# Streaming the projection matmuls from the last column to the first

## The chip, the core and the metric

One core of one Trainium2 chip runs the whole program in one launch. The metric is the device time of one execution in microseconds (us); lower is better. The kernel before was timed three times: 940.13, 941.47 and 944.43 us, median 941.47 us.

## The reference, cut to what matters

Two layers of a decoder trunk work on x, 256 tokens of 1024 features in float32. A layer is one wide projection of the normalised x, three token mixers, a gated merge, an output projection and a SwiGLU block:

```python
xn = rms(x, norm_mix_g)
z = xn @ w_in                                  # 1024 -> all heads and three gates
y_a, y_b, y_c = mlstm(z), sparse_attention(z), differential_attention(z)
merged = sum(sigmoid(gate_b) * (y_b @ w_branch[b]) for b in range(3))   # 512 -> 1024 each
x = x + merged @ w_out                         # 1024 -> 1024
g, u = split(rms(x, norm_ffn_g) @ w_gate_up)   # 1024 -> 2 x 2816
x = x + (silu(g) * u) @ w_down                 # 2816 -> 1024
```

Nearly all of the arithmetic is in the products with w_in, w_kv_up, w_branch, w_out, w_gate_up and w_down. They are called projections here.

## The kernel before

**Projections.** A float32 product is made of three passes of a faster matmul type (fp32r). Each operand is split into a high part (the fp32r copy) and a low part (the rest), and the passes are high by high, high by low and low by high, all summed in one PSUM tile. Two helpers issue these passes. `feat` (line 490) gives an output with features on partitions: the weight block of 128 columns is the stationary operand, and the 256 tokens of the activation's high or low part are streamed. `tok` (line 497) gives an output with tokens on partitions: 128 tokens of the activation are stationary, and 256, 332 or 512 weight columns are streamed. Every call writes the columns of a PSUM tile in the same order in which it streams them.

```python
490  def feat(ps, w, c0, a, first, last):
493      PE.matmul(ps, hi[:, c0:c0 + 128], a[:, 0, :], start=first, stop=False)
...
497  def tok(ps, w, c0, n, a, t, first, last):
501      PE.matmul(ps, a[:, 0, s], hi[:, c0:c0 + n], start=first, stop=False)
```

In the profile these are the matmuls `mm<-...`: `xg` and `fx` are the normalised inputs of a layer's two halves, `y` the mixers' outputs, `mg` the merged gates, `h` the SwiGLU activations and `ckv` the latent; `whi` and `wlo` are the two parts of a weight chunk. Matmuls named `at<-...` are the mixers' own (logits, transposes, values) and call neither helper.

**Weights.** `chunk` (line 472) loads up to 1024 columns of weights by one DMA on SyncE's queue into `raw`, makes `whi` on ScalarE and `wlo` on VectorE. Three buffers of each are in turn.

**Order of the work.** The kernel text only records operations. `Order.record` (line 149) notes for each which parts of which tiles it reads and writes, `Order.schedule` (line 177) lists them with a cost per instruction (`cost`, line 319) and a priority, and `Order.issue` (line 281) hands them to the engines in the order found. Line 288 issues every instruction, so every row of the profile has that line. A tile, or a part of one, is a `View` (line 20): a list of steps (index, rearrange, bitcast, broadcast) that `View.real` (line 94) applies to the real tile when the instruction is issued. `_next` (line 26) adds a step and passes on the shape and the range of columns.

**Readers of the PSUM tiles.** ScalarE or VectorE reads each finished `mm` tile as it always stands there, first column first; there are four such tiles in turn.

**Tiles of the second half.** In `norm` (line 509) the inputs of SwiGLU, `fx`, are written four feature blocks to one tile, each block as a high and a low part, so one tile has eight writers.

Of the kernel before, what the change touches and what calls it, by code (L numbers as in the profile page):

```python
# [19 lines left out]
class View:  # L20
    """A tile that is allocated when its first instruction is issued, or a part of it."""

# [65 lines left out]
    def bitcast(self, dtype):  # L88
        return self._next(("bitcast", dtype), self.shape, dtype)

    def to_broadcast(self, shape):
        return self._next(("bcast", shape), list(shape))

    def real(self, order):
        ap = order.tile_of(self.base)
        for s in self.steps:
            if s[0] == "get":
                ap = ap[s[1]]
            elif s[0] == "rearrange":
                ap = ap.rearrange(s[1], **s[2])  # L100
            elif s[0] == "bitcast":
                ap = ap.bitcast(s[1])
            else:
                ap = ap.to_broadcast(s[1])
        return ap
# [12 lines left out]
class Order:  # L118
    """Records instructions, puts them in an order by a list schedule, and issues them in it."""

# [186 lines left out]
def lat(a, b):  # L307
    """From the end of an instruction on engine a to the start of one on b that reads it, in us."""
    if a == b:
        return {"tensor": 0.0, "vector": 0.127, "scalar": 0.15, "gpsimd": 0.13, "sync": 0.0}[a]  # L310
    if b == "tensor":
        return 0.25
    return 0.2 if a == "tensor" or "gpsimd" in (a, b) else 0.14
# [5 lines left out]
def cost(op, views):  # L319
    """The time of an instruction in us."""  # L320
    n = max(math.prod(v.shape[1:]) for v in views)
    psum = any(v.base.psum for v in views)
    if op.eng == "tensor":
        n = math.prod(views[0].shape[1:])
        if op.fn == "transpose":
            return 0.109
        if views[1].dtype == BF16:
            return n / 1200
        if views[1].dtype == F32R:
            return max(n, 256) / 2400 + 0.0024  # L330
        return 0.216 if n <= 128 else 4 * n / 2400 + 0.0048
    if op.eng == "scalar":
        t = (0.05 if psum else 0.092) + n * 0.00084
        extra = [op.kw.get("scale"), op.kw.get("bias"), op.kw.get("accum_out")]
        return t + 0.093 * sum(isinstance(v, View) for v in extra)
    if op.eng == "vector":
        if op.fn == "reciprocal":
            return 0.05 + n * 0.0063
        t = 0.065 + n * (0.00052 if op.fn in ("tensor_copy", "tensor_scalar") and not psum else 0.00104)
        if op.fn == "scalar_tensor_tensor":  # L340
            t += 0.061 * isinstance(op.args[2], View)
        if op.fn == "tensor_tensor_reduce":
            t += 0.061 * isinstance(op.args[3], View)
        if op.fn == "tensor_scalar":
            t += 0.061 * sum(isinstance(v, View) for v in op.args[2:4])
        return t
    if op.eng == "gpsimd":
        if op.kw.get("op") == OP.pow:
            return 0.3 + n * 0.165
        if op.fn == "memset":  # L350
            return 0.04 + n * 0.0005
        if op.fn in ("tensor_scalar", "tensor_copy"):
            return 0.16 + n * (0.0037 if any(isinstance(v, View) for v in op.args[2:4]) else 0.00083)
        return 0.15 + n * 0.0021
    return 0.02 + 128 * n * 4 / 365e3
# [26 lines left out]
def plan():  # L382
    """The order in which a layer's weights are read: (array, row blocks, col blocks)."""
    seq = []
# [35 lines left out]
def kernel(ctx: ExitStack, tc: tile.TileContext, xT: bass.AP, wts: bass.AP, cst: bass.AP,  # L420
# [32 lines left out]

    # keeps TensorE's clock up until the first operands are there
    warm = S.tile([128, 256], BF16, name="warm")
# [34 lines left out]
    def feat(ps, w, c0, a, first, last):  # L490
        """ps [128 out, T] += w[:, c0:c0+128]^T a, three passes."""
        hi, lo = w
        PE.matmul(ps, hi[:, c0:c0 + 128], a[:, 0, :], start=first, stop=False)
        PE.matmul(ps, hi[:, c0:c0 + 128], a[:, 1, :], start=False, stop=False)
        PE.matmul(ps, lo[:, c0:c0 + 128], a[:, 0, :], start=False, stop=last)

    def tok(ps, w, c0, n, a, t, first, last):
        """ps [128 tok, n] += a[:, :, tile t]^T w[:, c0:c0+n], three passes."""
        hi, lo = w
        s = slice(t * 128, (t + 1) * 128)  # L500
        PE.matmul(ps, a[:, 0, s], hi[:, c0:c0 + n], start=first, stop=False)
        PE.matmul(ps, a[:, 0, s], lo[:, c0:c0 + n], start=False, stop=False)
        PE.matmul(ps, a[:, 1, s], hi[:, c0:c0 + n], start=False, stop=last)

    def rsqrt_cols(t, n):
        """t <- t ** -0.5 on GpSimd (t [128, n])."""
        G.tensor_tensor(t, t, mhalf[:, :n], op=OP.pow)

    def norm(gcol, wide, first=False):
        """x*g as hi/lo parts, 1/rms as token columns [128, 2] and as rows [128, T]."""  # L510
        xg = []
# [62 lines left out]
    def swap_halves(ap):  # L574
        """[128, h, 64] seen with the halves of the last axis exchanged, as two views."""
        return ap[:, :, 32:64], ap[:, :, 0:32]

    def rot(dst, z, nh, a, b):
        """dst = z * a + swap(z) * b over nh heads; a, b [128, 64]."""
        t2 = tmp([128, nh, 64], "rot")  # L580
        zh, zl = swap_halves(z)
        V.tensor_mul(t2[:, :, 0:32], zh, b[:, None, 0:32].to_broadcast([128, nh, 32]))
        V.tensor_mul(t2[:, :, 32:64], zl, b[:, None, 32:64].to_broadcast([128, nh, 32]))
        V.tensor_mul(dst, z, a[:, None, :].to_broadcast([128, nh, 64]))
        V.tensor_add(dst, dst, t2)
# [10 lines left out]
    def qk_heads(z, t, ab, dstT, query):  # L596
        """z [128 tok, 512] -> per-head RMS, RoPE, transposed into dstT[:, :, tile t]. Of a query
        the 1/rms is returned instead, as columns scaled by -1/sqrt(64), for softmax."""
        sq = tmp([128, 8, 64], "sq")
# [19 lines left out]
    def softmax(t, heads, qT, kT, bias, scale):  # L619
        """exp(logits - max) of the heads, [128 q, len(heads), nk], and its row sums."""  # L620
        n, nk = len(heads), 128 * (t + 1)
# [15 lines left out]
    def keyT(p, n, t):  # L637
        """p [128 q, n, nk] -> [128 keys, n, key tile, 128 q]."""
        ps = atps([128, n, t + 1, 128])
        for i in range(n):  # L640
            for kt in range(t + 1):
                PE.transpose(ps[:, i, kt, :], p[:, i, kt * 128:(kt + 1) * 128], ident)
        r = tmp([128, n, t + 1, 128], "pT")
        A.activation(r, ps, AF.Copy)
        return r

    def parts(dst, ps, t, g=None):
        """hi/lo of ps [128, 4, 128] (scaled by g[:, k]) into dst[:, k, :, tile t]."""
        s = slice(t * 128, (t + 1) * 128)
# [10 lines left out]
    for li in range(L):  # L660
# [12 lines left out]
        S.margin = True  # L673
        # mLSTM q and k: projection, causal convolution, silu
        mqk = []
# [19 lines left out]

        # DSA latent
        ps = [mmps([128, 256]) for _ in range(2)]
# [28 lines left out]

        # indexer projections and mLSTM gates
        ps2 = [mmps([128, 332]) for _ in range(2)]
# [26 lines left out]

        # index scores and the top-k mask
        bias = []
# [23 lines left out]

        # DSA queries
        def proj512():
# [13 lines left out]

        # DSA keys and values
        skT = S.tile([128, 4, T], F32, tag="qT", name="skT", bufs=4)
# [13 lines left out]

        # DSA attention
        y = [S.tile([128, 4, 2, T], F32R, tag="y", name=f"y{b}", bufs=3) for b in range(3)]
# [17 lines left out]

        # differential attention
        p = tmp([128, 2, 64], "lamp")
# [60 lines left out]

        # mLSTM gates
        mf = mif[:, :, 4:8]
# [33 lines left out]
        for t in range(2):  # L932
# [8 lines left out]
            if t == 1:  # L941
# [3 lines left out]
                ET.append(u)  # L945
        # (s tile, t tile) blocks: (0, 0), (1, 1), (0, 1)
        for b, (si, ti) in enumerate(((0, 0), (1, 1), (0, 1))):
# [5 lines left out]

        # mLSTM values and output gate
        p = proj512()
# [42 lines left out]

        # branch gates
        gt = []  # L1000
# [14 lines left out]
        S.margin = False  # L1015
        # branch projections, gated and merged
        mg = []
# [22 lines left out]

        # output projection
        for e in range(8):
# [5 lines left out]

        # SwiGLU
        xg, rcol, rB = norm(c[:, C_NF:C_NF + 8], True)  # L1050
# [50 lines left out]
def _layout(inp):  # L1101
    """The inputs in the kernel's layouts (moves only)."""
    src = {"in": inp["w_in"], "kv": inp["dsa_w_kv_up"], "out": inp["w_out"], "gu": inp["w_gate_up"],
# [42 lines left out]
```

## Time and profile before

| what | value |
|---|---|
| three runs | 940.13, 941.47, 944.43 us; median 941.47 us |
| the profiled execution's own time: span from first to last instruction (what lies around the span was not listed) | 942.7 us |
| TensorE matmul busy; weight loads busy | 933.5 us (99%); 888.6 us (94%) |
| VectorE, ScalarE, GpSimd busy | 678.6 us (72%), 534.0 us (57%), 103.3 us (11%) |
| matmul instructions, weight loads | 7154, 7154 |
| read from HBM, rate over the span | 158.27 MB, 169 GB/s |
| granted TensorE clock, mean | 1.000 |

The profile's busy time of an engine is the union of its instructions' times. Matmuls overlap each other, since a row's duration runs from the first column entering to the last one landing, so the pace of matmuls is read from the distance between their starts and not from their mean duration. The chain of waits is the path followed back from the last instruction; what stands in it sets the end.

### The profile page before, as it was taken

How to read it: one execution, taken by the hardware profiler on the slowest of the kernel's cores; microseconds unless marked ns; L12 is line 12 of the kernel's file. 1: busy time of each engine (PE TensorE's matmuls, PEld its weight loads, DVE VectorE, ACT ScalarE, POOL GpSimd, SP SyncE). 2: the span in 40 equal slices, each digit the busy share in tenths (PEclk: the TensorE clock that was granted, in tenths of full speed). 3: DMA queues.
4: the chain of work that ended last, by engine and by line, in shares of the span. 5: the costliest groups of instructions: out<-in, count | busy, mean ns of one | idle time of the engine just before them, and what ended most of it. 6: DMA issues, size and time to landing. Idle time of an engine off the chain costs nothing.

```text
span 942.7 us, 18057 instructions
## 1 busy us (share of the span) xinstructions
PE 933.5 (99%) x7154; PEld 888.6 (94%) x7154; DVE 678.6 (72%) x1268; ACT 534.0 (57%) x927; POOL 103.3 (11%) x149
## 2 busy tenths in 40 slices
PE   8999999999999999999999999999999999999998
PEld 7988779999999999999999787899999999999998
DVE  6889988765886666665578898796669866666553
ACT  5686667774365444444457767577644655445432
POOL 5002431110011000001110121213000300000000
PEclk9999999999999999999999999999999999999999
DMA  6655433445555555555555453333555555555663
GB/s 222 203 188 179 154 100 106 131 163 187 186 179 181 189 191 181 188 181 186 186 184 184 157 193 121 112 113 118 176 187 192 178 180 185 194 181 186 193 198 96
DMA packets 46821, 160.49 MB, mean 170 GB/s; under 512 B 5392, under 2 KB 7568, under 8 KB 46736
## 3 DMA queue, kind: packets, MB, share of 16 engines
q1 hardware_dynamic: 46736, 159.34, 52.0%
q8 instruction: 56, 0.92, 0.4%
q14 instruction: 29, 0.24, 0.1%
HBM read 158.27 MB, written 1.05 MB: 169 GB/s over the span
## 4 chain that ended last, share of the span: by engine, by line
PE 98%; DVE 1%; DMA 0%; issue 0%; SPq 0%; ACT 0%
PE mm L288 89%; PE at L288 8%; DVE e L288 0%; DMA x<-in_xT_dram 0%; DVE xg L288 0%; SPq L288 0%; DVE zr L288 0%; ACT xg L288 0%; DVE dn L288 0%; DVE x L288 0%; DVE rot L288 0%; ACT nsq L288 0%; DVE wlo L288 0%; DVE mn L288 0%; DVE cf L288 0%
## 5 line engine op out<-in xcount | busy, mean ns | idle before, releaser
L288 ACT ACTIVATE whi<-raw 128x1024 fp32r<-128x1024 f32 (+2 forms) x303 | 315.9, 1043 | 332.9 <-PE mm L288 212.0
L288 DVE TENSOR_TENSOR wlo<-raw,whi 128x1024 fp32r<-128x1024 f32 (+2 forms) x303 | 365.4, 1207 | 184.0 <-ACT whi L288 182.2
L288 PE MATMUL mm<-fx,whi 128*128 128x256 f32 x1408 | 249.6, 279 | 0.0
L288 PEld LDWEIGHTS mm<-fx,whi 128*128 128x128 f32 x1408 | 215.2, 188 | 0.0
L288 PE MATMUL mm<-xg,whi 128*128 128x256 f32 x1024 | 195.2, 289 | 1.8 <-DVE xg L288 1.8
L288 PE MATMUL mm<-fx,wlo 128*128 128x256 f32 x704 | 196.8, 280 | 0.0
L288 PEld LDWEIGHTS mm<-xg,whi 128*128 128x128 f32 x1024 | 163.7, 195 | 3.3 <-DVE xg L288 2.6
L288 PE MATMUL mm<-whi,xg 128*128 128x512 f32 (+2 forms) x512 | 150.3, 373 | 0.0
L288 PE MATMUL mm<-xg,wlo 128*128 128x256 f32 x512 | 148.0, 289 | 0.6 <-DVE wlo L288 0.6
L288 PEld LDWEIGHTS mm<-fx,wlo 128*128 128x128 f32 x704 | 132.0, 188 | 0.0
L288 PE MATMUL mm<-h,whi 128*128 128x256 f32 x704 | 124.5, 280 | 0.0
L288 PEld LDWEIGHTS mm<-h,whi 128*128 128x128 f32 x704 | 107.7, 188 | 0.0
L288 PEld LDWEIGHTS mm<-whi,xg 128*128 128x128 f32 x512 | 92.1, 188 | 14.7 <-issue 1.0
L288 PEld LDWEIGHTS mm<-xg,wlo 128*128 128x128 f32 x512 | 99.7, 195 | 1.2 <-DVE wlo L288 0.9
L288 PE MATMUL mm<-h,wlo 128*128 128x256 f32 x352 | 98.6, 280 | 0.0
L288 PE MATMUL mm<-wlo,xg 128*128 128x512 f32 (+2 forms) x256 | 95.6, 374 | 0.0
L288 PE MATMUL mm<-y,whi 128*128 128x256 f32 x384 | 67.9, 280 | 0.0
L288 PEld LDWEIGHTS mm<-h,wlo 128*128 128x128 f32 x352 | 66.4, 189 | 0.0
L288 POOL TENSOR_TENSOR nacc<-nacc,nsq 128x256 f32<-128x256 f32 x28 | 26.3, 939 | 361.1 <-ACT nsq L288 222.5
L288 PEld LDWEIGHTS mm<-y,whi 128*128 128x128 f32 x384 | 58.6, 187 | 0.0
L288 PEld LDWEIGHTS mm<-wlo,xg 128*128 128x128 f32 x256 | 48.3, 189 | 7.7 <-issue 0.7
L288 PE MATMUL mm<-y,wlo 128*128 128x256 f32 x192 | 53.6, 279 | 0.0
(193 smaller groups left out, 1095.4 us busy)
## 6 DMA issues: line engine op xcount, KB each, us to landing
raw<-in_wts_dram SPq DMA_DIRECT2D x279, 512.0 KB, 3.7
raw<-in_wts_dram SPq DMA_DIRECT2D x16, 384.0 KB, 3.9
raw<-in_wts_dram SPq DMA_DIRECT2D x4, 498.0 KB, 3.6
x<-in_xT_dram SPq DMA_DIRECT2D x4, 256.0 KB, 4.4
out_dram<-x SPq DMA_DIRECT2D x8, 128.0 KB, 3.4
row<-in_rows_dram SPq DMA_DIRECT2D x2, 388.0 KB, 5.7
raw<-in_wts_dram SPq DMA_DIRECT2D x2, 332.0 KB, 2.9
raw<-in_wts_dram SPq DMA_DIRECT2D x2, 256.0 KB, 3.8
```

Source lines behind the costliest of these rows:

```text
L288: getattr(getattr(nc, o.eng), o.fn)(*args, **kw)
```

## The change

`View` gets a method that turns the order of the columns round, and both helpers apply it to the streamed operand and to the PSUM output of all three passes. The stationary operands stay as they are. Streamed column j still lands in output column j; only the order in time goes from the last column to the first. Docstrings and comments are dropped as well, and no instruction is added or removed.

```diff
@@ class View
+    def back(self):
+
+        return self._next(("back",), self.shape)
@@ View.real
+            elif s[0] == "back":
+                ap = ap[:, ::-1]
@@ feat
         hi, lo = w
-        PE.matmul(ps, hi[:, c0:c0 + 128], a[:, 0, :], start=first, stop=False)
-        PE.matmul(ps, hi[:, c0:c0 + 128], a[:, 1, :], start=False, stop=False)
-        PE.matmul(ps, lo[:, c0:c0 + 128], a[:, 0, :], start=False, stop=last)
+        ps, a0, a1 = ps.back(), a[:, 0, :].back(), a[:, 1, :].back()
+        PE.matmul(ps, hi[:, c0:c0 + 128], a0, start=first, stop=False)
+        PE.matmul(ps, hi[:, c0:c0 + 128], a1, start=False, stop=False)
+        PE.matmul(ps, lo[:, c0:c0 + 128], a0, start=False, stop=last)
@@ tok
         hi, lo = w
         s = slice(t * 128, (t + 1) * 128)
-        PE.matmul(ps, a[:, 0, s], hi[:, c0:c0 + n], start=first, stop=False)
-        PE.matmul(ps, a[:, 0, s], lo[:, c0:c0 + n], start=False, stop=False)
-        PE.matmul(ps, a[:, 1, s], hi[:, c0:c0 + n], start=False, stop=last)
+        ps, h, l = ps.back(), hi[:, c0:c0 + n].back(), lo[:, c0:c0 + n].back()
+        PE.matmul(ps, a[:, 0, s], h, start=first, stop=False)
+        PE.matmul(ps, a[:, 0, s], l, start=False, stop=False)
+        PE.matmul(ps, a[:, 1, s], h, start=False, stop=last)
```

## Rows read from the trace of the kernel before

**Rows 1.** The page's first two parts: busy time of TensorE's matmuls and weight loads and of the other engines, with instructions; then the clock granted to TensorE in 40 equal slices of the span, in tenths (9 is 90% or more).

```profile
PE 933.5 (99%) x7154; PEld 888.6 (94%) x7154; DVE 678.6 (72%) x1268; ACT 534.0 (57%) x927; POOL 103.3 (11%) x149
...
PEclk9999999999999999999999999999999999999999
```

**Rows 2.** The page's chain that ended last, as shares of the span: by engine, and its first lines by line and tile.

```profile
PE 98%; DVE 1%; DMA 0%; issue 0%; SPq 0%; ACT 0%
PE mm L288 89%; PE at L288 8%; DVE e L288 0%; DMA x<-in_xT_dram 0%; DVE xg L288 0%; SPq L288 0%; DVE zr L288 0%; ACT xg L288 0%; DVE dn L288 0%; DVE x L288 0%; DVE rot L288 0%; ACT nsq L288 0%; DVE wlo L288 0%; DVE mn L288 0%; DVE cf L288 0%
```

**Rows 3.** All that TensorE waited for in the span: who, total us, times, longest us.

```profile
PE at L288 <- ACT warm L288: 2.3, 1, 2.3
PE mm L288 <- DVE xg L288: 1.8, 2, 1.2
PE mm L288 <- DVE wlo L288: 0.6, 1, 0.6
PE at L288 <- DVE mn L288: 0.3, 1, 0.3
```

**Rows 4.** The groups of projection matmuls over the span, each shape apart: stationary columns, streamed columns, count, then busy us and mean ns of one, then idle time before.

```profile
L288 PE MATMUL mm<-fx,whi 128*128 128x256 f32 x1408 | 249.6, 279 | 0.0
L288 PE MATMUL mm<-fx,wlo 128*128 128x256 f32 x704 | 196.8, 280 | 0.0
L288 PE MATMUL mm<-xg,whi 128*128 128x256 f32 x1024 | 195.2, 289 | 1.8 <-DVE xg L288 1.8
L288 PE MATMUL mm<-xg,wlo 128*128 128x256 f32 x512 | 148.0, 289 | 0.6 <-DVE wlo L288 0.6
L288 PE MATMUL mm<-h,whi 128*128 128x256 f32 x704 | 124.5, 280 | 0.0
L288 PE MATMUL mm<-whi,xg 128*128 128x512 f32 x384 | 124.0, 397 | 0.0
L288 PE MATMUL mm<-h,wlo 128*128 128x256 f32 x352 | 98.6, 280 | 0.0
L288 PE MATMUL mm<-wlo,xg 128*128 128x512 f32 x192 | 76.6, 399 | 0.0
L288 PE MATMUL mm<-y,whi 128*128 128x256 f32 x384 | 67.9, 280 | 0.0
L288 PE MATMUL mm<-y,wlo 128*128 128x256 f32 x192 | 53.6, 279 | 0.0
L288 PE MATMUL mm<-mg,whi 128*128 128x256 f32 x256 | 46.0, 283 | 0.0
L288 PE MATMUL mm<-mg,wlo 128*128 128x256 f32 x128 | 35.6, 283 | 0.0
L288 PE MATMUL mm<-whi,xg 128*128 128x332 f32 x64 | 15.1, 317 | 0.0
...
L288 PE MATMUL mm<-whi,xg 128*128 128x256 f32 x64 | 11.8, 283 | 0.0
L288 PE MATMUL mm<-whi,ckv 128*128 128x512 f32 x32 | 11.0, 404 | 0.0
...
L288 PE MATMUL mm<-wlo,xg 128*128 128x332 f32 x32 | 10.0, 313 | 0.0
L288 PE MATMUL mm<-wlo,xg 128*128 128x256 f32 x32 | 9.1, 283 | 0.0
...
L288 PE MATMUL mm<-wlo,ckv 128*128 128x512 f32 x16 | 6.4, 401 | 0.0
```

**Rows 5.** The chain of waits in order of time: start us, length us, what, how many matmuls. The first stretch has matmuls of 512 streamed columns, the other two (SwiGLU of layer 0 and of layer 1) of 256.

```profile
68.48 28.88 PE mm L288 x127
...
293.44 185.66 PE mm L288 x1574
...
756.74 181.89 PE mm L288 x1545
```

**Rows 6.** TensorE in order of time, the first of three matmuls of 332 columns, and then the first of the next three: start us, length us, instruction, count.

```profile
49.71 0.31 PE L288 MATMUL mm<-wlo,xg 128*128 128x332 f32 x1
...
50.16 0.31 PE L288 MATMUL mm<-wlo,xg 128*128 128x332 f32 x1
```

**Rows 7.** TensorE in order of time near the start, matmuls of 256 columns: the first row's two and one left out, the next row's two and one left out, and the one after them.

```profile
8.37 0.63 PE L288 MATMUL mm<-xg,whi 128*128 128x256 f32 x2
...
9.01 0.63 PE L288 MATMUL mm<-xg,whi 128*128 128x256 f32 x2
...
9.65 0.41 PE L288 MATMUL mm<-xg,whi 128*128 128x256 f32 x1
```

**Rows 8.** TensorE in order of time: four transposes of 128 columns, first those of `mM`, where the operand is one column repeated 128 times, then those of `yn`, where it is 128 different columns.

```profile
173.33 0.60 PE L288 MATMUL at<-K,mM 128*128 128x128 f32 x4
...
193.69 0.60 PE L288 MATMUL at<-K,yn 128*128 128x128 f32 x4
```

**Rows 9.** All engines in order of time at the start of layer 0's SwiGLU: the first matmuls that read `fx`, and VectorE's last write of a part of `fx`.

```profile
287.88 0.40 PE L288 MATMUL mm<-fx,whi 128*128 128x256 f32 x2
...
290.24 0.96 DVE L288 SCALAR_TENSOR_TENSOR fx<-x,col,fx 128x256 fp32r<-128x256 f32 x1
```

**Rows 10.** The costliest group of the page: ScalarE's making of `whi`, busy us and mean ns, then its idle time before and who ended most of it.

```profile
L288 ACT ACTIVATE whi<-raw 128x1024 fp32r<-128x1024 f32 (+2 forms) x303 | 315.9, 1043 | 332.9 <-PE mm L288 212.0
```

## The prediction

> **What bounds the kernel now.** I read the page's busy line first. TensorE's matmuls fill 99% of the span, its weight loads 94%, VectorE 72%, ScalarE 57% [rows 1]. A busy share alone proves little, since matmul rows overlap, so I went on to the chain that ended last: 98% of it is TensorE, 89% in the projection matmuls `mm` and 8% in the mixers' `at` [rows 2]. Then the waits: in the whole span TensorE waits 2.3 + 1.8 + 0.6 + 0.3 = 5.0 us for anyone [rows 3]. So the end is set by how fast TensorE gets through its stream, and nothing covers a change of pace there: a nanosecond more per projection matmul is a nanosecond more of the end, times their number.
>
> That number comes from the view that groups instructions by shape [rows 4]. Of 256 streamed columns there are 1408 + 704 + 1024 + 512 + 704 + 352 + 384 + 192 + 256 + 128 + 64 + 32 = 5760 matmuls, of 512 columns 384 + 192 + 32 + 16 = 624, and of 332 columns 64 + 32 = 96: 6480 in all. All of them come from the two helpers, so the change touches every one.
>
> The pace is read from the long unbroken stretches of the chain. 256 columns: 185.66 / 1574 = 118.0 ns and 181.89 / 1545 = 117.7 ns; I take 118.0. 512 columns: 28.88 / 127 = 227.4 ns [rows 5]. 332 columns: three from 49.71 to 50.16 us, 150 ns each [rows 6]. A straight line through the first and the last has (227.4 - 118.0) / 256 = 0.427 ns per column and 118.0 - 256 x 0.427 = 8.7 ns that come once per matmul; for 332 columns it gives 8.7 + 141.8 = 150.5 ns, which fits. So it is the number of streamed columns that sets the pace, with a small fixed part. The projections take 5760 x 118.0 + 624 x 227.4 + 96 x 150 ns = 679.7 + 141.9 + 14.4 = 836 us, near the chain's 89% of 942.7 us (839 us). [...]
>
> **The change part by part.** *Instructions, order and edits of text.* The docstrings and comments issue nothing. `back` adds a step to a view and passes on its shape and range of columns; the planner's cost is worked out from shapes, its dependences from ranges. So the order, the queues, the DMAs and the counts stay: 0 us, and no cover is needed, because nothing is added.
>
> *The arithmetic.* Streamed and output columns are turned round together, so each sum lands where it did, and the readers of PSUM start, as before, when the last pass ends. A reader that starts at column 0 doesn't start earlier because that column is written last. 0 us.
>
> *Waits.* Should a turned view be taken for more of its tile than it covers, a matmul would wait for all writers of that tile. For most operands that is so already, or all parts are long written. The place with a price is the start of SwiGLU, where four blocks share a tile: the first matmul on `fx` starts at 287.88 us, the fifth block's turn comes 12 matmuls later at 287.88 + 12 x 0.118 = 289.30 us, and VectorE's last part is there at 290.24 + 0.96 = 291.20 us [rows 9]. The wait would be 1.9 us, in two layers 3.8 us. Behind it the rest of TensorE's queue would stand, and VectorE and ScalarE would wait for `mm`.
>
> *The pace of a turned stream.* This is the only term of weight, and no row of this trace has an operand with a step of minus one on any engine. Lower end: if the 8.7 ns fixed part were owed to the ascending order and vanished, 6480 x 8.7 ns = 56 us would be gained. Upper end: the same matmul form runs slower near the start of this very trace, six of 256 columns from 8.37 to 9.65 us, 213 ns each or 0.833 ns per column [rows 7], about half the later rate; why is left open here, I take only the pace. At 0.833 ns per column the matmuls take 213, 427 and 277 ns: more by 95, 199 and 127 ns, in all 5760 x 95 + 624 x 199 + 96 x 127 ns = 547 + 124 + 12 = 683 us, less some 4 us for those of the start that have that pace already: 679 us. Value taken: 0. The nearest row for an operand that isn't 128 neighbours in rising order is that of the transposes: four with one column repeated 128 times take 0.60 us, and four with 128 different columns take 0.60 us [rows 8]. The step of the columns did not matter there. It is a weak witness, as (0.60 - 0.27) / 3 = 0.11 us for 128 columns is the half rate of the start and not 0.427 ns per column, and its step is 0. [...]
>
> [...]
>
> *Sum.* 0 + 0 + 0 + 0. The profiled execution has a span of 942.7 us, 1.2 us above the median of the three runs (941.47), so the forecast on the runs' scale is 941.5 us.
>
> **The rivals.** *Halved stream (slower).* [...] Price 679 us, time 941.5 + 679 = 1620 us. ScalarE and VectorE, which already wait for `mm` (212 us before the `whi` group alone [rows 10]), would only wait longer.
>
> [...]
>
> *Wider waits.* 3.8 us as above: 945 us, within what a measurement tells from no change. Against: the range of columns is handed on.
>
> *The fixed part goes (faster).* 886 us. For it: weight loads and streams walk rising addresses together, and 94% of the span has a load in flight [rows 1]. Against: they read different tiles in both helpers.
>
> *The change does nothing.* If both turned patterns were put back in rising order before they reach the chip, the time is 941.5 us too; only the traces' equality would show, not which of the two it was.
>
> **How the numbers follow.** About 0.5% of the time, 4.7 us, is what a measurement of this kernel can tell from no change. No change of pace, including the edit that does nothing: 0.55. Wider waits: 0.03, also inside 0.5%. Halved stream: 0.20; I add 0.04 for a stream slower still. A second fixed part or another price up to a few times that: 0.13. Faster: 0.05. So same 0.58, slower 0.37, faster 0.05. The likeliest case's own range is 938 to 946 us, from the spread of the runs and the wider waits. Without the halved stream and what lies beyond (0.24) and the faster case, too little would be held, so the range goes up to it: 937 to 1625 us.
>
> **What would show it.** Right: the stretches of SwiGLU again at 118 ns per matmul, single rows of 0.28 us, `mm` at 89% of the chain, and the same counts. Wrong: rows of 0.41 us like those of the start and 213 ns per matmul mean the halved stream. A pace of some 127 ns at 256 columns with an equal addition at 512 means a fixed part. A new wait of `mm` for VectorE's `fx` means wider waits.

## The result, and the profile after

The changed kernel is slower by about one per cent: 950.57 us (950.36 to 951.65, 5 runs) against 941.47 us (936.33 to 944.57, 5 runs), ratio 1.0101, interval [1.006, 1.0142]. The runs of before lie at several levels some 4.5 us apart and those of the changed kernel at one; beside runs of before that all lie at the upper level, the changed kernel is 0.7% slower (last experiment). The profiled executions differ by 948.7 - 942.7 = 6.0 us of span.

The page of the changed kernel answers to [rows 1] and [rows 2] with the same picture, and so do its waits to [rows 3]. First the busy line and the chain's shares:

```profile
PE 938.5 (99%) x7154; PEld 890.5 (94%) x7154; DVE 678.7 (72%) x1268; ACT 534.0 (56%) x927; POOL 103.4 (11%) x149
...
PE 97%; DVE 1%; DMA 0%; issue 0%; POOL 0%; SPq 0%
```

```profile
PE mm L294 <- DVE xg L294: 2.6, 2, 1.4
PE at L294 <- ACT warm L294: 2.3, 1, 2.3
PE mm L294 <- DVE wlo L294: 0.7, 1, 0.7
PE at L294 <- DVE mn L294: 0.3, 1, 0.3
```

The counts are the same, each engine's instructions stand in the same order, and TensorE waits 5.9 us for others instead of 5.0. The 0.9 us more lie in the first 18 us, and they cost nothing in the end: the first long stretch of the changed kernel starts at 18.73 us, that of before at 18.88. The granted clock is 1.00 in both from 18 us on; the means, 1.000 and 0.996, differ by the first 18 us alone (1.00 and 0.81 there), and a second trace of before with the mean 0.996 has the same span (first experiment). So the six us are in TensorE's pace. The chain in order of time shows them (start us, length us, matmuls). These are its long stretches in the changed kernel, in the program's order: q and k of the mixers (xg streamed), 512 weight columns, gates to output projection of layer 0 (xg, then y, then mg), SwiGLU of layer 0 (fx, then h), and the last two again for layer 1:

```profile
18.73 31.67 PE mm L294 x253
...
68.18 29.63 PE mm L294 x127
...
201.30 90.33 PE mm L294 x759
...
293.94 187.99 PE mm L294 x1574
...
670.46 87.49 PE mm L294 x735
...
760.26 184.40 PE mm L294 x1545
```

The same view of the kernel before, for the stretches that [rows 5] does not have:

```profile
18.88 31.99 PE mm L288 x253
...
200.72 90.39 PE mm L288 x759
...
666.91 87.51 PE mm L288 x735
```

SwiGLU grew by 2.3 and 2.5 us and the 512-column stretch by 0.75 us, but q and k became 0.3 us shorter and the stretches from the gates on stayed. The groups by shape say it by operand (busy us, then mean ns of one); of before in [rows 4]: fx 279, xg 289, 512 columns 397, mg 283 ns.

```profile
L294 PE MATMUL mm<-fx,whi 128*128 128x256 f32 x1408 | 254.3, 282 | 0.0
...
L294 PE MATMUL mm<-xg,whi 128*128 128x256 f32 x1024 | 192.1, 287 | 2.7 <-DVE xg L294 2.6
...
L294 PE MATMUL mm<-whi,xg 128*128 128x512 f32 x384 | 126.2, 404 | 0.0
...
L294 PE MATMUL mm<-mg,whi 128*128 128x256 f32 x256 | 45.4, 282 | 0.0
```

Fx went up and mg and xg went down. Distances between starts are sharper. In order of time, twelve matmuls on fx from 300.97 to 302.41 us, 120.0 ns each, in the changed kernel:

```profile
300.97 0.40 PE L294 MATMUL mm<-fx,whi 128*128 128x256 f32 x2
...
302.41 0.40 PE L294 MATMUL mm<-fx,whi 128*128 128x256 f32 x2
```

and twelve from 301.05 to 302.46 us, 117.5 ns each, in the kernel before:

```profile
301.05 0.40 PE L288 MATMUL mm<-fx,whi 128*128 128x256 f32 x2
...
302.46 0.40 PE L288 MATMUL mm<-fx,whi 128*128 128x256 f32 x2
```

Taken over the whole trace, from the start times of neighbouring matmuls of one kind (distances over 171 ns at 256 columns and over 341 ns at 512 left out), the mean distance in ns is:

| streamed | count | before | after | all of them, us |
|---|---|---|---|---|
| fx, 256 | 2112 | 117.78 | 119.99 | +4.7 |
| y, 256 | 576 | 117.79 | 119.98 | +1.3 |
| h, 256 | 1056 | 117.82 | 118.12 | +0.3 |
| xg, 256 | 1536 | 119.81 | 118.38 | -2.2 |
| mg, 256 | 384 | 120.01 | 118.35 | -0.6 |
| weights against xg, 256 | 96 | 120.00 | 118.31 | -0.2 |
| weights against xg, 512 | 576 | 234.37 (median 227) | 239.23 (median 233) | +2.8 |

The sum is +6.1 us; the spans differ by 6.0. (332 columns stayed at 151.8 and 151.9 ns.) One change of direction made some streams slower and others faster, by operand. The operands also differ in where they lie, which the tile addresses of the built program tell and no trace does: counted from the weight blocks, in bytes within a partition modulo 256, xg and mg lie at 0, fx, y and ckv at 64, and h at every multiple of 32. "At 64" is short for this below; a stream that goes from the first column to the last is called rising, the other turned.

### The profile page after: what moved, and what is told of

Its sections match the earlier page's. It is cut to its first block, busy times and chain, and to the rows that moved or that the text cites. A ratio compares the mean times of both kernels' runs of the same rounds, so it can differ in the third digit from the quotient of the medians.

```text
span 948.7 us, 18047 instructions
## 1 busy us (share of the span) xinstructions
PE 938.5 (99%) x7154; PEld 890.5 (94%) x7154; DVE 678.7 (72%) x1268; ACT 534.0 (56%) x927; POOL 103.4 (11%) x149
## 4 chain that ended last, share of the span: by engine, by line
PE 97%; DVE 1%; DMA 0%; issue 0%; POOL 0%; SPq 0%
PE mm L294 89%; PE at L294 8%; DMA x<-in_xT_dram 0%; DVE e L294 0%; DVE xg L294 0%; POOL rcol L294 0%; SPq L294 0%; DVE wlo L294 0%; DVE zr L294 0%; DVE dn L294 0%; DVE x L294 0%; DVE rot L294 0%; DVE rcol L294 0%; DVE mn L294 0%; DVE cf L294 0%
## 5 line engine op out<-in xcount | busy, mean ns | idle before, releaser
L294 PE MATMUL mm<-fx,whi 128*128 128x256 f32 x1408 | 254.3, 282 | 0.0
L294 PE MATMUL mm<-xg,whi 128*128 128x256 f32 x1024 | 192.1, 287 | 2.7 <-DVE xg L294 2.6
L294 PEld LDWEIGHTS mm<-xg,whi 128*128 128x128 f32 x1024 | 160.4, 190 | 4.3 <-DVE xg L294 3.6
L294 PE MATMUL mm<-whi,xg 128*128 128x512 f32 (+2 forms) x512 | 152.3, 378 | 0.0
L294 PEld LDWEIGHTS mm<-xg,wlo 128*128 128x128 f32 x512 | 97.3, 190 | 1.3 <-DVE wlo L294 0.9
```

The source lines that it names most:

```text
L294: getattr(getattr(nc, o.eng), o.fn)(*args, **kw)
```

## The experiments

Theory A: a stream's pace depends on how its read falls against the read of the next weight block, so on the distance between the two places and on the direction. Rivals: B, a fixed price of descending order at one port; C, a state of one execution; D, the stage and the engines beside it; E, the place of the streamed tile alone.

**The kernel before, a second time** (no edit).

> The kernel before, unchanged, profiled a second time. In its first trace the mean distance between two starts of 256-column projection matmuls was 117.8 ns where fx or y is streamed, 117.8 where h is, 119.8 where xg is, 120.0 where mg is; with 512 weight columns streamed the median was 227 ns. Theory A (meeting of two reads: what sets these is where the streamed operand lies against the weight block that is being loaded, and the direction of the stream): the same five numbers within 0.3 ns, and a span within a few us of 942.7. Theory B (a price of the descending order itself at one port): also the same. Theory C (the numbers are a state of one execution, drawn anew each time): other numbers, for instance 120 for fx and 118 for xg. The ratio to the kernel before is 1.000 and its interval is the yardstick for the others; the spread of 936 to 945 us in the runs of before should show up again.

944.82 us against 944.83, ratio 1.0001 [0.9992, 1.0011], span 942.8 us. Fx 117.78, h 117.82, xg 119.81, mg 120.01 ns, median 227 ns: what A and B ask for is there, and C in its plain form falls. The expected spread did not show: ten and seventeen runs all lay between 943.4 and 945.7 us.

**Only feat turned**, tok as before:

```diff
-        ps, h, l = ps.back(), hi[:, c0:c0 + n].back(), lo[:, c0:c0 + n].back()
+        h, l = hi[:, c0:c0 + n], lo[:, c0:c0 + n]
```

> Only feat's streams and outputs are turned, tok's stay rising. Theory A and B: in feat the changed kernel's pace (fx and y 120.0 ns, xg and mg 118.4, h 118.1), in tok that of before (median 227 ns at 512 columns). Sum against the trace of before: fx 2112 x 2.2, y 576 x 2.2, h 1056 x 0.3, xg 1536 x -1.4, mg 384 x -1.7 ns = 4.6 + 1.3 + 0.3 - 2.2 - 0.6 = +3.4 us, span 946.1 us. Theory C: any of 936 to 950 us, and paces that don't follow the direction.

948.29 us, ratio 1.0032 [1.0019, 1.0045], span 946.7 us: +3.9 us against the second trace of before, +3.4 expected. In the chain, 512 columns have the length of before and SwiGLU that of the changed kernel:

```profile
68.76 28.91 PE mm L294 x127
...
293.29 187.98 PE mm L294 x1574
```

**Only tok turned**, feat as before:

```diff
-        ps, a0, a1 = ps.back(), a[:, 0, :].back(), a[:, 1, :].back()
+        a0, a1 = a[:, 0, :], a[:, 1, :]
```

> Only tok's streams and outputs are turned, feat's stay rising. Theory A and B: median 233 ns instead of 227 at 512 columns, 624 x 4.9 ns = +3.1 us, span 945.8 us, and feat's paces as before (fx 117.8, xg 119.8 ns). With e2 the two parts should add up to the 6.0 us between the spans of the two first traces. Theory C: no such sum.

947.59 us, ratio 1.0030 [1.0019, 1.0041], span 945.4 us (+2.6, +3.1 expected). The same two stretches have changed sides:

```profile
68.53 29.64 PE mm L294 x127
...
294.76 185.67 PE mm L294 x1574
```

The two parts add up: 3.9 + 2.6 = 6.5 us of span, 6.2 us by the second trace of before and that of the changed kernel run again (949.0, below).

**Only the stream turned, and only the PSUM output turned**, in both helpers.

```diff
-        ps, a0, a1 = ps.back(), a[:, 0, :].back(), a[:, 1, :].back()
+        a0, a1 = a[:, 0, :].back(), a[:, 1, :].back()        # stream only
+        ps, a0, a1 = ps.back(), a[:, 0, :], a[:, 1, :]       # output only
```

> The streamed operand is turned in all projections and the PSUM output rises again, so the columns of every projection come out in the wrong order; the instructions and their number stay. Theory A (the streamed read is what matters): the changed kernel's paces, fx 120.0, xg 118.4, 512 columns 233 ns, span about 948.7 us. Theory B with the price at the PSUM write: the paces of before, fx 117.8, xg 119.8, 512 columns 227 ns, span about 942.7 us.

> The PSUM output is turned in all projections and the streamed operand rises again, so the columns of every projection come out in the wrong order. Theory A (the streamed read against the weight load's read): the paces of before, fx and y 117.8 ns, xg 119.8, mg 120.0, median 227 ns at 512 columns, span 942.8 us. Theory B (a price at the PSUM write): with the stream-only kernel already at the changed kernel's paces, some addition here, up to 6 us.

Stream only: 951.10 us, 1.0063 [1.0046, 1.0079], span 949.5 us; fx 119.99, xg 118.36, median 233 ns, all as in the changed kernel. Output only: 940.55 us, 0.9999 [0.9969, 1.0030]; y 117.79, xg 119.81, mg 120.02, median 227 ns as before. So no price at the PSUM write shows, and the direction of the streamed read alone makes the whole difference. But the span was 939.0 us, not 942.8. The chain of the output-only kernel shows why:

```profile
294.19 185.67 PE mm L294 x1574
...
757.54 177.38 PE mm L294 x1545
```

SwiGLU of layer 0 has the length of [rows 5], that of layer 1 is 4.5 us shorter: fx has 113.5 ns per matmul there on average, the first 36 distances 117.8 ns and the others, to the end of fx, 113.3. The pace changes right behind an interruption, two transposes of `rcol`; six matmuls on fx take 0.71 us ahead of them and 0.68 us behind:

```profile
755.98 0.40 PE L294 MATMUL mm<-fx,whi 128*128 128x256 f32 x2
...
756.69 0.40 PE L294 MATMUL mm<-fx,whi 128*128 128x256 f32 x2
...
757.16 0.38 PE L294 MATMUL at<-K,rcol 128*128 128x128 f32 x2
...
757.61 0.39 PE L294 MATMUL mm<-fx,whi 128*128 128x256 f32 x2
...
758.29 0.39 PE L294 MATMUL mm<-fx,whi 128*128 128x256 f32 x2
```

So a rising stream at 64 has two paces. The trace of before has the same interruption at 756.36 us and goes on at 117.8 ns, so it doesn't always change the pace. Two paces in one layer's fx would also account for the levels in the runs of before: 22 of them, beside this kernel's, lay near 944.8, 940 and 935.5 us, steps of 1056 x 4.3 ns = 4.5 us, the price of one layer's fx. The run of this kernel that was profiled is one of the middle level. Of before itself no run of a lower level was traced.

**Xg and mg moved to 64**, everything rising. Unused gaps ahead of and behind a tile's slots move it and leave the rest where it was modulo 256:

```diff
+PADS = {"xg": (64, 192)}        # bytes ahead of and behind the tag's slots
 ...
+            if not b.psum and b.tag not in self.placed:
+                self.pad(self.tail)
+                ...
```

> The kernel before, rising in everything; only the tiles xg and mg lie 64 bytes further on in each partition (an unused gap ahead of them, another behind them so that all else keeps its place modulo 256). Then xg and mg lie as fx and y do in the kernel before: 64 bytes past a multiple of 256 from the weight blocks, instead of 0. Theory A: xg and mg go from 119.8 and 120.0 to 117.8 ns, 1536 x 2.0 + 384 x 2.2 ns = 3.9 us less, span about 938.9 us, plus or minus what the 512-column matmuls do, whose stationary blocks are moved too (between 227 and 233 ns as seen so far, up to 3.8 us either way). Theory D (the paces belong to the stage and the engines working beside it, not to the place): xg stays at 119.8 and mg at 120.0, span 942.8 us.

Span 941.2 us. Mg has 117.78 ns, xg 117.78 in layer 0 and 116.86 in layer 1 (where some hundred and fifty near its start, again right behind transposes of `rcol`, stood at 113 to 114): the paces of fx, so D falls. What was gained there (1536 x 2.4 + 384 x 2.2 ns = 4.5 us) was partly given back by the 512 columns against xg, median 233 ns and 5 ns more on the mean, 576 x 5 ns = 2.9 us. The streamed weights lie at 192 from the xg block that is loaded there, instead of 0. The time, 942.87 us, is 1.0018 [0.9996, 1.0041] of before, whose runs were partly at the lower levels. The groups by shape show mg at 279 ns, the value that fx has in [rows 4], and 512 columns at 401:

```profile
L301 PE MATMUL mm<-whi,xg 128*128 128x512 f32 x384 | 125.6, 401 | 0.0
...
L301 PE MATMUL mm<-mg,whi 128*128 128x256 f32 x256 | 45.2, 279 | 0.0
```

**The changed kernel with fx, y and ckv moved to 0** (`PADS = {"y": (192, 64)}`, the tag of all three).

> The changed kernel, with only the tiles of fx, y and ckv moved so that they lie 0 past a multiple of 256 bytes from the weight blocks, as xg and mg do, instead of 64. Theory A: fx and y go from 120.0 to the 118.4 ns that xg and mg have there when turned, 2688 x 1.6 ns = 4.3 us less, span 948.7 - 4.3 = 944.4 us; xg, mg and the 512-column matmuls stay at 118.4, 118.4 and 233 ns. Theory D: 120.0 ns and 948.7 us as in the changed kernel.

Fx and y at 118.34 and 118.33 ns, xg, mg and 512 columns as in the changed kernel, span 943.8 us (944.4 expected). That is the fastest of seven runs; their median is 946.94 us, some 4 us below the changed kernel's 950.57 and 951.00, and 1.0067 [1.0041, 1.0092] of before, whose runs were partly at the lower levels. SwiGLU of both layers is 1.7 us shorter than in the changed kernel:

```profile
292.89 186.30 PE mm L307 x1574
...
757.03 182.71 PE mm L307 x1545
```

**All five at 192**, rising (`PADS = {"xg": (192, 64), "y": (128, 128)}`), run on two chips.

> The kernel before, rising in everything, with xg, mg, fx, y and ckv all 192 bytes past a multiple of 256 from the weight blocks. In the trace of before only some blocks of h lie so: 144 matmuls with 115.5 ns on average against 117.8 for all of h. Theory A with that average taken as the pace of a steady stream: fx and y 2688 x 2.3 ns and xg and mg 1920 x 4.4 ns, 6.2 + 8.4 = 14.6 us less, span about 928 us; if the 115.5 ns owe something to the neighbours of those matmuls in h, less of it, but still other numbers than 117.8 and 119.8. Theory D: 942.8 us.

> The rising kernel with xg, mg, fx, y and ckv at 192 once more. Two states at 192: if no 256-column stream but h's fell into the faster one, 942.8 - 1920 x 2.1 ns = 938.8 us of span less what the 512-column matmuls do; if all did, 4.5 us less for fx of each layer and more for the others. 927 to 938 us, and several levels among its runs; faster than both kernels in every run.

First 929.73 us, 0.9896 [0.9858, 0.9934], span 930.7 us; then 937.99 us, 0.9927 [0.9912, 0.9942], span 936.1 us: faster than all runs of before beside it each time. In the first trace fx of layer 0 and y and mg of layer 1 stood at 113.3 to 113.5 ns, the others of these at 117.7 to 117.8; in the second all of these stood at 117.8. SwiGLU of layer 0 and of layer 1 in the chain of the first run:

```profile
291.05 180.78 PE mm L301 x1573
...
744.74 181.89 PE mm L301 x1545
```

and in that of the second:

```profile
289.98 185.66 PE mm L301 x1574
...
750.12 181.89 PE mm L301 x1545
```

The expected 928 us took one mean for what is a mix of two paces, so that the first run came near it and the second did not. Several levels were expected among the second's runs, but its four lay between 937.87 and 938.26 us. In the first, fx of layer 1 began in the faster pace and left it at the transposes of `rcol`.

**Only the weight parts moved**, by 64, rising (`PADS = {"whi": (64, 0), "wlo": (0, 192)}`).

> The kernel before, rising in everything; only the weight parts whi and wlo lie 64 bytes further on, all else where it was modulo 256. Counted from the weight blocks, fx, y and ckv now lie at 0 (modulo 256 bytes) instead of 64, and xg and mg at 192 instead of 0. Theory A (the distance between the two reads counts): fx and y go from 117.8 to the 120.0 ns of a rising stream at 0, 2688 x 2.2 = 5.9 us more; xg and mg go from 119.9 to 117.8 or 113.4 ns, the two states seen at 192, 1920 x 2.1 to 6.5 = 4.0 to 12.5 us less; 512 columns about 229 ns at the median, as in the kernel with all at 192. Span 936 to 945 us. Theory E (where the streamed tile itself lies counts, not the distance): fx and y 117.8 and xg and mg 119.9 ns as before.

Fx 119.96 and y 119.97 ns, mg 113.43, xg 115.84 and 116.37 by layer, median 230 ns, span 940.9 us; 943.62 us, 0.9986 [0.9977, 0.9995]. Fx, y, xg and mg themselves stayed where they were, and fx took the pace that xg and mg had had. E falls: the distance counts. ScalarE's and VectorE's writes of `whi` and `wlo` moved as well, but they don't set the pace: in the kernel before, fx stood at 117.83 ns with a write of `whi` under way and at 117.75 without, at 117.81 with one of `wlo` and at 117.76 without. SwiGLU has the length that it has in the changed kernel, though every stream rises:

```profile
289.92 187.97 PE mm L301 x1574
...
752.46 184.32 PE mm L301 x1545
```

and mg, among the groups by shape, has the shortest rows of all kernels:

```profile
L301 PE MATMUL mm<-mg,whi 128*128 128x256 f32 x256 | 43.5, 276 | 0.0
```

**The changed kernel, again** (no edit).

> The changed kernel, unchanged, beside the kernel before on one chip. Theory A with two states: its runs lie close together, 950 to 952 us, since a turned stream at 64 has shown 120.0 ns alone; the runs of the kernel before lie at any of three levels some 4.5 us apart (1056 matmuls on fx in a layer x 4.3 ns), near 944.7, 940.2 and 935.6 us, so that the ratio comes out between 1.006 (all at the upper level) and 1.016 (all at the lowest), with the levels of before deciding where.

951.00 us (950.4 to 951.8) against 945.00 (943.9 to 945.6): ratio 1.0066 [1.0049, 1.0082], span 949.0 us, fx 119.99 ns. With all runs of before at their upper level the change costs 6.0 us. The first measurement's 9.1 us has some 3 us more because runs of before lay lower.

## Why the prediction was right or wrong

**Instructions, order, waits, arithmetic: 0 us.** Right. Counts and order are the same, and the chain's shares within one per cent. Wider waits did not come: fx does not appear among TensorE's waits.

**What bounds it.** Right, and it mattered: since nothing covers a change of pace, 2.2 ns on a 118 ns matmul reached the end in full.

**The pace of a turned stream: value taken 0.** This step failed. The likeliest case's own range, 938 to 946 us, did not hold the time. The wide one did by luck: it had been drawn up to 1625 us for a halved stream that did not come, and the outcome "slower", with 0.37, rested mostly on that stream as well. The one row beside the 0, that of the transposes [rows 8], has a step of 0, so the 0 for a turned stream was the author's judgement, and no run shows it. The runs showed in its place that the turned read costs 2.2 ns of 117.8 on fx and 6 of 227 at 512 columns (6.6 ns against the faster pace of fx), not a halved rate, while xg and mg gain 1.4 and 1.7 ns; with only the output turned the distances were those of before (y 117.79, xg 119.81, mg 120.02 ns) or, for fx of layer 1, shorter (113.5 ns). What the estimate left out is where the weight blocks lie, which TensorE loads nearly all the time, 89.9 of 90 us in the gates' stretch (201 to 291 us) of the kernel before. The price goes by the distance of the stream from them: at 64 a rising stream has 117.8 or 113.4 ns and a turned one 120.0; at 0 it is 120.0 rising and 118.4 turned.

**One pace for all 256-column matmuls.** The 118.0 ns of the prediction came from SwiGLU and was put on all 5760. [Rows 4] already said otherwise: mg at 283 ns and fx at 279 for the same shape, at the same clock. Had that been followed up, the operands could have been told apart before. The "8.7 ns once per matmul" is not a constant either: it went from about 4 to 11 ns with the place (113.4 and 120.0 ns less 256 x 0.427). The sum's scale was off too: in all listed runs the time is some 1.8 us above the span, so the profiled span of 942.7 us belongs to the run of 944.43 us, the slowest of the three, and not to one near the median.

**The rivals.** The halved stream is out: a turned stream of 256 columns had 118.1 to 120.0 ns, nothing near 213. The second fixed part had the right sign and a size six to nine times too large (8.7 ns on each of 6480 matmuls, 56 us, against 6 to 9), but a price on every matmul can't make xg and mg faster, and these gained 1.4 and 1.7 ns. "The fixed part goes" was set aside since load and stream "read different tiles in both helpers". That objection did not hold: moving the weight blocks alone by 64 bytes took fx, which lies in another tile, from 117.8 to 120.0 ns.

**What stays open.** Why distance and direction count is not shown: no row has a meeting of the two reads. What puts a rising stream at 64 or 192 into the faster pace is not known. In the traces fx changed its pace only at or a few matmuls behind an interruption by other matmuls, but not at every one. One program stood at 929.73 us on one chip and at 937.99 us on another, and the runs of before lay at three levels on the first of these and at one on the second; what is the chip's and what is chance can't be told apart from these runs. The rule for 512 columns is open as well: there a rising stream had a median of 227 ns at 0, 229 to 230 at 64 and 233 at 192, so that 0 was best and not worst.

## What to carry to other kernels

Where TensorE's stream sets the end, compare the distance between starts of matmuls of one shape across operands: here a spread of a few ns came from where the operands lie, and 0.7 to 1.0% could be had without touching the arithmetic, by unused gaps of 64 to 192 bytes. Judge an edit of access order by operand and not by the total, since gains and losses cancel (the stretch of 759 matmuls moved by 0.06 us while each matmul on y in it took 2.2 ns more and each on xg and mg 1.4 and 1.7 ns less). When the runs of an unchanged kernel lie at levels, look for stretches with two paces before reading a ratio of one per cent.

## What the runs showed of the hardware that was not expected

A steady stream of 256-column fp32r matmuls, each with its own weight load, ran at 120.0, 118.4, 117.8 or 113.4 ns per matmul with the same instructions, at a granted clock of 1.00 in every stretch from 51 us on of the six traces where it was read. Distance (modulo 256 bytes) and direction picked among them: rising at 0 gave 120.0; turned at 0, 118.4; rising at 64 or 192, 117.8 or 113.4; turned at 64, 120.0. Of the two paces at 64 and 192, fx kept the one in which it went on behind the last interruption for a thousand matmuls, to the end of its layer, while xg changed between them within a layer. A turned PSUM output showed no cost (117.8 and 120.0 ns for y and mg, as rising).
